# A written instruction order for ScalarE and VectorE, square sums moved to VectorE, and decay sums in fp32r, in a hybrid decoder step

## The chip, the cores and the metric

The kernel runs on one core of one Trainium2 chip. The metric is device time in microseconds. The engines are TensorE (PE, with its weight loads as PEld), VectorE (DVE), ScalarE (ACT), GpSimd (POOL) and SyncE (SP), which here only issues DMAs; ScalarE issues DMAs too.

## What is computed

One inference step of a hybrid autoregressive layer, for two groups that share the weights: a prompt of 256 tokens, and 8 samples of 8 tokens each with 1024 past positions in a paged cache. Model width is 1024, so 320 token columns pass through every projection.

```python
x += W_out[concat(MoBA heads, Mamba-2 SSD heads)](rmsnorm(x))
x += cross_attention(rmsnorm(x), rmsnorm(mem))
x += squared_relu_mlp(rmsnorm(x))

rmsnorm(x, g) = x * rsqrt(mean(x * x) + eps) * g

# Mamba-2 part, per chunk, with da = -dt * exp(a_log)
cum    = cumsum(da)
decay  = exp(where(causal, cum[l] - cum[s], -inf))
scores = einsum(C[l], B[s]) * decay
```

The step returns the outputs of both groups and the new keys, values, convolution rows, recurrent states and memory keys and values.

## The kernel before

All activations lie transposed, 128 model rows on the partitions and the 320 tokens in the free dimension. A weight chunk is 128x1024 fp32 (512 KB). `load` (L280) brings it in, on SyncE's queue or, for chunks 5 to 47, on ScalarE's. `chunk` splits it into a high part `wh` (ScalarE copy to fp32r, L332) and a low part `wl` (VectorE subtract, L333). The activations are split the same way by `split` (ScalarE L474, VectorE L475). `gemm3` (L338 to L340) then makes each product of three fp32r matmuls: high by high, high by low, low by high. Three raw, three high and three low chunk buffers exist, and two PSUM banks named `mm` for the gemms.

The program has a first part, in which many streams share TensorE, and a second, the MLP, which is gemms nearly throughout. The streams of the first part are: V and Q (value, query and key projections), F (their norms), S and T (sample and prompt attention), B and Z (convolution input and gate), D and R (the SSD scan), N (gated norm), O and J (the two halves of the output projection, `oa` and `os`), M, K and W (memory norms, keys and values), X (factors of the cross attention), a to d (cross attention), and G (its query and output projection, `ox`). Each stream is a generator; the string `ORDER` names, letter by letter, whose next piece is emitted, and that fixes TensorE's order. For the other engines the tile scheduler picks an order by priorities, when the program is built; on the chip each engine then runs its own list strictly in order.

Three places matter here.

- **Square sums.** A norm needs the sum of squares over 1024 model rows. `gather` (L433) squares each of the eight 128-row tiles on ScalarE (`square`, L423) and adds seven of them to the first on GpSimd, into `acc`. `means` (L442) copies the last 64 columns to fill the third 128-column tile (L439, GpSimd), then sums over the partitions with small matmuls. There are four such sums: of the input `x`, of the memory, of `x` after the output projection, and of `x` after the cross attention.
- **Decay sums.** `ssd_mix` (L997) scales a triangular matrix by each head's `da` into `rr`, on ScalarE, and one fp32 matmul for each 512 columns (L1013) against `gt` gives the differences of cumulative sums; ScalarE exponentiates them (L1014). The two prompt chunks have 1024 columns each, the sample chunk 512: five matmuls.
- **Row sums.** `sums` (L448) sums squares of heads by matmul, `rows_out` (L453) copies them out, and `transpose` (L316) turns them.

In the output projections the results leave PSUM on VectorE with the residual (`mix_done` L1268, `residual` L1282).

Of the kernel before, what the change touches and what calls it, by code (L numbers as in the profile page):

```python
# [47 lines left out]
for _n, _c in (("g_mix", 8), ("g_x", 8), ("g_mem", 8), ("g_mlp", 8), ("g_ssm", 4),  # L48
# [21 lines left out]
ORDER = ("VVVVQQQQQQQFQVQQQFQQVFVQQQQFQFQQQQFVQQQSSQQSQFQSQQQZQSSFSFSSSFFBFBSBBSBBZBBZBBSTZSSSBBBTBSSTBTBBBSBS"  # L70
         "BBSBSSBBSSSVTSSTZZSBBBSSTBZTBBBSSTBSSSZSDZDSTZDSDZDSSSDBDZDSSDZDDSSZZSDTSDDZRSSRSSRSSROMWROWRORROROO"
         "MNOOWZONONOWOOONONNOWOJJJJJJJJJJJMJJJWKJJKGWKKKKKKKJKKKKKKKaXMMGGGGGGMGGGGGGWGMGGGOcMXXbaaXccbaXdacb"
         "babcbaccddacddKbacddGGGGGGGGGGGGWGGGGG")
# [60 lines left out]
def _layout(a):  # L134
# [45 lines left out]
    for n, s in (("qg", f["q_norm_g"][0]), ("kg", f["k_norm_g"][0])):  # L180
# [12 lines left out]
        "ssm_s": (NB, P, 512), "mkT": (P, 4, 256), "mvo": (256, 512)}  # L193


def _body(tc, nc, I, O):
# [475 lines left out]
    def dt_part(tp):  # L672
# [26 lines left out]
        return dt, da  # L699
# [291 lines left out]
    def ssd_mix(t, bs_, tri, gt, n, out):  # L991
# [665 lines left out]
    for m in range(8):  # L1657
# [7 lines left out]
        S.dma_start(O["yT"][:, m, :], xT[:, m, :])  # L1665
    stD.close()
# [29 lines left out]
```

## Time and profile before

| | us |
|---|---|
| three runs | 532.46, 533.10, 533.56 (median 533.1) |
| the profiled execution | 533.69 |
| its span, first to last instruction | 531.9 |
| TensorE busy | 509.5 (96%) |
| VectorE busy | 342.5 (64%) |
| ScalarE busy | 251.9 (47%) |
| GpSimd busy | 79.2 (15%) |

The profile comes from one execution. TensorE's busy time is of pipelined matmuls with modelled ends, so overlapping lengths are listed longer than the step from one to the next. An idle time stands with the instruction that ended it, and with the releaser that came last. A tile name stands without its number, and a line number can be that of a helper that many places call.

### The profile page before, as it was taken

The numbers are of one execution on the slowest core, as the hardware profiler recorded it, in microseconds if no ns is written. First come the engines' busy times: TensorE is split into PE (matmuls) and PEld (weight loads), VectorE is DVE, ScalarE is ACT, GpSimd is POOL, SyncE is SP. The second block draws the span as 40 slices with busy tenths as digits, with TensorE's granted clock in tenths as the row PEclk, the third lists the DMA queues.
The fourth block names the chain that finished last, engine by engine and source line by source line (L and its number), as shares of the span: only waits on it lengthen the run. The fifth ranks groups of instructions, "written<-read, shape, count | busy, mean of one in ns | idle before, by whom it ended". The sixth has DMA issues, their size and how long they took to land.

```text
span 531.9 us, 10547 instructions
## 1 busy us (share of the span) xinstructions
PE 509.5 (96%) x3954; PEld 457.4 (86%) x3954; DVE 342.5 (64%) x677; ACT 251.9 (47%) x509; POOL 79.2 (15%) x126
## 2 busy tenths in 40 slices
PE   8899988999999999989899899999999999999997
PEld 6888577768667699879678899999999999999997
DVE  6858788677667788854647769776766533444331
ACT  8433536856666845552585443433433333223320
POOL 4700000110100310320002322322212100000000
PEclk9999999999999999998999899999999999999999
DMA  8799997979998235775942348464744455544530
GB/s 292 254 348 388 371 323 273 369 265 357 316 390 332 100 120 167 248 282 180 332 180 57 102 132 304 159 210 148 226 136 153 160 171 155 156 163 171 164 100 12
DMA packets 45365, 116.54 MB, mean 219 GB/s; under 512 B 5058, under 2 KB 7234, under 8 KB 45314
## 3 DMA queue, kind: packets, MB, share of 16 engines
q1 hardware_dynamic: 39266, 94.37, 52.0%
q10 hardware_dynamic: 6048, 21.50, 11.2%
q8 instruction: 31, 0.51, 0.4%
q14 instruction: 20, 0.16, 0.1%
HBM read 109.71 MB, written 6.14 MB: 218 GB/s over the span
## 4 chain that ended last, share of the span: by engine, by line
PE 80%; DVE 8%; ACT 7%; DMA 2%; issue 2%; SPq 1%; POOL 0%; ACTq 0%; DVEq 0%; POOLq 0%
PE mm L338 21%; PE mm L339 20%; PE mm L340 20%; ACT wh L332 3%; DVE wl L333 2%; PE sc L812 2%; PE as L865 2%; DVE big L475 2%; PE ms L316 2%; PE as L316 1%; PE sc L653 1%; DMA p<-memT 1%; DMA big<-xT 1%; PE as L1530 1%; PE as L1506 1%
## 5 line engine op out<-in xcount | busy, mean ns | idle before, releaser
L332 ACT ACTIVATE wh<-wr 128x1024 fp32r<-128x1024 f32 (+1 forms) x115 | 119.1, 1037 | 196.0 <-PE mm L339 128.2
L333 DVE TENSOR_TENSOR wl<-wr,wh 128x1024 fp32r<-128x1024 f32 (+1 forms) x115 | 146.0, 1272 | 95.8 <-ACT wh L332 94.4
L338 PE MATMUL mm<-big,wh 128*128 128x320 f32 x544 | 174.9, 322 | 3.2 <-DVE x2T L1282 1.4
L340 PE MATMUL mm<-big,wl 128*128 128x320 f32 x544 | 169.2, 311 | 1.4 <-DVE wl L333 1.4
L339 PE MATMUL mm<-big,wh 128*128 128x320 f32 x544 | 169.3, 311 | 0.0
L338 PEld LDWEIGHTS mm<-big,wh 128*128 128x128 f32 x544 | 103.3, 190 | 12.5 <-issue 8.7
L340 PEld LDWEIGHTS mm<-big,wl 128*128 128x128 f32 x544 | 103.4, 190 | 1.6 <-DVE wl L333 1.6
L339 PEld LDWEIGHTS mm<-big,wh 128*128 128x128 f32 x544 | 103.4, 190 | 0.6 <-issue 0.2
L340 PE MATMUL mm<-hh,wl 128*128 128x320 f32 x256 | 78.9, 308 | 0.0
L339 PE MATMUL mm<-hl,wh 128*128 128x320 f32 x256 | 78.9, 308 | 0.0
L338 PE MATMUL mm<-hh,wh 128*128 128x320 f32 x256 | 78.9, 308 | 0.0
L338 PEld LDWEIGHTS mm<-hh,wh 128*128 128x128 f32 x256 | 48.0, 188 | 0.0
L340 PEld LDWEIGHTS mm<-hh,wl 128*128 128x128 f32 x256 | 48.0, 188 | 0.0
L339 PEld LDWEIGHTS mm<-hl,wh 128*128 128x128 f32 x256 | 48.0, 188 | 0.0
L1619 POOL TENSOR_TENSOR t<-t 128x320 f32<-128x320 f32 x32 | 29.2, 912 | 88.1 <-DVE t L1616 79.2
L433 POOL TENSOR_TENSOR acc<-acc,sq 128x320 f32<-128x320 f32 x14 | 15.8, 1132 | 93.6 <-ACT sq L423 93.2
L1616 DVE SCALAR_TENSOR_TENSOR t<-mm,rb 128x320 f32<-128x320 f32 x32 | 15.6, 489 | 14.7 <-PE mm L340 13.6
L433 POOL TENSOR_TENSOR acc<-acc,t 128x320 f32<-128x320 f32 (+1 forms) x14 | 13.9, 995 | 41.5 <-ACT t L423 41.0
L1620 DVE TENSOR_TENSOR hl<-t,hh 128x320 fp32r<-128x320 f32 x32 | 15.4, 482 | 4.6 <-POOL t L1619 4.6
L812 PE MATMUL sc<-kv,qs 128*32 128x256 f32 x256 | 16.8, 382 | 0.2 <-DVE qs L602 0.2
L1617 ACT ACTIVATE hh<-t 128x320 fp32r<-128x320 f32 x32 | 14.7, 458 | 4.2 <-DVE t L1616 4.1
L865 PE MATMUL as<-kv,p 128*32 128x256 f32 x256 | 15.9, 382 | 0.0
(353 smaller groups left out, 635.7 us busy)
## 6 DMA issues: line engine op xcount, KB each, us to landing
wr<-w SPq DMA_DIRECT2D x69, 512.0 KB, 3.5
wr<-w ACTq DMA_DIRECT2D x41, 512.0 KB, 4.5
kv<-ckT SPq DMA_DIRECT2D x64, 256.0 KB, 5.1
kv<-cv SPq DMA_DIRECT2D x64, 256.0 KB, 5.9
kv<-mk SPq DMA_DIRECT2D x8, 512.0 KB, 4.4
kv<-mv SPq DMA_DIRECT2D x8, 512.0 KB, 5.0
kv<-h SPq DMA_DIRECT2D x4, 512.0 KB, 7.6
big<-h SPq DMA_DIRECT2D x4, 512.0 KB, 5.6
```

The source lines that it names most:

```text
L316: PE.transpose(out, in_, ident[:n, :n])
L332: A.activation(hi[:, c], raw[:, c], AF.Copy)
L333: V.tensor_tensor(lo[:, c], raw[:, c], hi[:, c], op=ALU.subtract)
L338: PE.matmul(out, hi[:, cols], xh, start=start, stop=False)
L339: PE.matmul(out, hi[:, cols], xl, start=False, stop=False)
L340: PE.matmul(out, lo[:, cols], xh, start=False, stop=stop)
L433: G.tensor_tensor(a, a, square(x, sq and sq()), op=ALU.add)
L812: PE.matmul(ps[r:r + 32, 256 * n:256 * n + 256], qs[:, s, g, b0 + e, :], kbs[e][:, :, 128 * (2 * g + s):128 * (2 * g + s) + 128], start=s ...
L865: PE.matmul(yv[r:r + 32, 0:256], pT[:, 2 * n + q, r:r + 32], vbs[e][:, q, 256 * g:256 * g + 256], start=n == 0 and q == 0, stop=first and ...
L1616: V.scalar_tensor_tensor(t, ps[:, :T], 0.0, rb3, op0=ALU.max, op1=ALU.mult)
L1619: G.tensor_tensor(f, t, t, op=ALU.mult)
L1620: V.tensor_tensor(hl[:, m, :], f, hh[:, m, :], op=ALU.subtract)
```

## The change

Five edits.

1. `ACT_ORDER` and `DVE_ORDER` list the places of all of ScalarE's and VectorE's instructions in the emitted program, DMA issues of ScalarE included ("3+1" is 3 and 4). At the end of `_body`, `_issue_order` ties each instruction to the one before it in the list, so that the scheduler must issue them so. SyncE and GpSimd stay with the scheduler.
2. `ORDER` is a new string: the pieces of TensorE's work come in another order.
3. `gather` adds on VectorE instead of GpSimd: 28 adds.
4. The padding of `acc` to 384 columns is a memset to 1 on GpSimd before the first square; for the input `x`, VectorE copies the last 64 columns.
5. In `ssd_mix`, `da` is split into `dah` and `dal`; ScalarE scales the triangular matrix by the high part (`rh`), VectorE by the low part (`rl`, one instruction for 512 columns), and two fp32r matmuls that accumulate take the place of each fp32 one. The halves of a prompt chunk are made one after the other, in two buffers; `gt` is copied to fp32r.

```diff
-ORDER = ("VVVVQQQQQQQFQVQQQFQQVFVQQQQFQFQQQQFVQQQSSQQSQFQSQQQZQSSFSFSSSFFBFBSBBSBBZBBZBBSTZSSSBBBTBSSTBTBBBSBS"
+ORDER = ("VVFVVQQQQQQQQQQQQQQQVFVQFVQFFQQQQFVQQQQQSSQQQFSSQQZQZQSSFSFSSSFFBBBBSZBBSBBFSBBTZSBSSBBBSSTBBTBTBBSS"
...
+ACT_ORDER = ("1 0 2 19 3+1 20 6 5 7 21 8+3 22 12+3 23 16+2 24+2 28 30 33 32 27 37 34 29 43 38 31 50 39 44 36 35 53 59 40+1 "
...
+DVE_ORDER = ("0+2 17 4 3 5 18 6+7 19 14+1 20 16 21+2 27 32 24 35 25+1 36 28 30 29 31 53 33+1 37 39 38 40+8 54 73 49 51 50 52 "
...
+def _issue_order(tc, nc, eng, runs):
+    ins = [i for i in nc.cur_bb.bb.instructions if i.engine == eng and i.is_tile_traced]
+    ins = [ins[i] for i in _runs(runs)]
+    info = mybir.DependencyInfo(mybir.DependencyClass.NoSync, mybir.DependencyReason.DATA)
+    for a, b in zip(ins, ins[1:]):
+        tc.add_manual_dep(b, a.name, info, reason="issue order")
...
     def gather(acc, x, sq=None):
         if not acc:
+            n = x.shape[-1]
             acc.append(tl(tp_, [P, 384], "acc", bufs=2))
-            square(x, acc[0][:, :x.shape[-1]])
+            if n % P:
+                G.memset(acc[0][:, n:P * -(-n // P)], 1.0)
+            square(x, acc[0][:, :n])
         else:
             a = acc[0][:, :x.shape[-1]]
-            G.tensor_tensor(a, a, square(x, sq and sq()), op=ALU.add)
+            V.tensor_tensor(a, a, square(x, sq and sq()), op=ALU.add)
...
-        if n % P:
-            G.tensor_copy(a[:, n:P * nt], a[:, n - 64:n])
...
     def x_squares():
         for kt in range(8):
             gather(xsq, xT[:, kt, :], lambda: tm(T))
+        V.tensor_copy(xsq[0][:, T:], xsq[0][:, TP:T])
...
+        dah, dal = [tl(p1, [P, 24], n, F32R) for n in ("dah", "dal")]
+        V.tensor_copy(dah, da)
+        V.tensor_tensor(dal, da, dah, op=ALU.subtract)
...
-        for h in range(8):
-            A.activation(rr[:, h, :], tri, AF.Copy, scale=dat[:, h:h + 1])
+        gtr = tl(made["sb"], [P, P], "es", F32R)
+        A.activation(gtr, gt, AF.Copy)
+        hn = 512 // n
+        def expand(h0):
+            rh, rl = [tl(made["sb"], [P, hn, n], "rx", F32R, bufs=2) for _ in range(2)]
+            for h in range(hn):
+                A.activation(rh[:, h, :], tri, AF.Copy, scale=dah[:, h0 + h:h0 + h + 1])
+            V.tensor_tensor(rl, tri[:, None, :].broadcast_to((P, hn, n)), dal[:, h0:h0 + hn, None].broadcast_to((P, hn, n)), op=ALU.mult)
+            return rh, rl
+        rx = expand(0)
...
-        for c in range(0, 8 * n, 512):
+        for h in range(0, 8, hn):
+            if h:
+                rx = expand(h)
+                yield 0.5, 2.0
             sg = ms()
-            PE.matmul(sg, gt, rf[:, c:c + 512], start=True, stop=True)
-            A.activation(df[:, c:c + 512], sg, AF.Exp)
+            for i, r in enumerate(rx):
+                PE.matmul(sg, gtr, r.rearrange("p h l -> p (h l)"), start=i == 0, stop=i == 1)
+            A.activation(rr[:, h:h + hn, :], sg.rearrange("p (h l) -> p h l", h=hn), AF.Exp)
...
+    for eng, runs in ((mybir.EngineType.Activation, ACT_ORDER), (mybir.EngineType.DVE, DVE_ORDER)):
+        if runs:
+            _issue_order(tc, nc, eng, runs)
```

Line numbers of the changed program are higher by 35 to 70: L333 becomes L384, L442 L494, L448 L500, L475 L527, L720 L776, L1282 L1349.

VectorE at the end of the `ox` stage, before: `x2T` is the residual, `wl` the low part of the next weight chunk, `big` the low part of the split.

```order
L475 SCALAR_TENSOR_TENSOR big_3735<-x2T_2845,prm_81,big_3735 128x320
L1282 TENSOR_TENSOR x2T_2845<-mm_3873,qs_2526 128x320
L1282 TENSOR_TENSOR x2T_2845<-mm_3892,kv_2527 128x320
L333 TENSOR_TENSOR wl_4020<-wr_4017,wh_4019 128x1024
L475 SCALAR_TENSOR_TENSOR big_3735<-x2T_2845,prm_81,big_3735 128x320 x2
L443 TENSOR_SCALAR ti_3938<-ms_3940 128x3
```

And in the changed program, where `acc` is the square sum:

```order
L1349 TENSOR_TENSOR x2T_2880<-mm_3902,qs_2533 128x320
L527 SCALAR_TENSOR_TENSOR big_3763<-x2T_2880,prm_81,big_3763 128x320
L1349 TENSOR_TENSOR x2T_2880<-mm_3921,kv_2534 128x320
L487 TENSOR_TENSOR acc_3786<-acc_3786,sq_3918 128x320
L384 TENSOR_TENSOR wl_4048<-wr_4045,wh_4047 128x1024
L487 TENSOR_TENSOR acc_3786<-acc_3786,sq_3937 128x320
L527 SCALAR_TENSOR_TENSOR big_3763<-x2T_2880,prm_81,big_3763 128x320 x2
L495 TENSOR_SCALAR ti_3967<-ms_3968 128x3
```

The adds stand between residual, low part and the last two splits, which are last in both.

TensorE at the end of the memory keys, before: the last gemm matmuls on `kv`, the square sum's matmuls, the row sums of the key squares `t`, and the transposes of their copy `s`.

```order
L339 MATMUL mm_3183<-kv_2555,wh_3186 128x256
L340 MATMUL mm_3183<-kv_2554,wl_3187 128x256
L442 MATMUL ms_3227<-cst_82,acc_2903 128x8 x3
L448 MATMUL ms_3234<-t_3214,cst_82 32x256
L448 MATMUL ms_3234<-t_3180,cst_82 32x256
L448 MATMUL ms_3234<-t_3146,cst_82 32x256
L448 MATMUL ms_3234<-t_3112,cst_82 32x256
L316 MATMUL ms_3241<-cst_82,s_578_3239 128x128 x2
L338 MATMUL mm_3260<-big_2900,wh_3263 128x320
L339 MATMUL mm_3260<-big_2900,wh_3263 128x320
```

And in the changed program (`sc` is the memory value projection W):

```order
L1549 MATMUL sc_2582<-wh_3235,kv_2552 128x512
L1550 MATMUL sc_2582<-wl_3236,kv_2552 128x512
L1551 MATMUL sc_2582<-wh_3235,kv_2553 128x512
L1549 MATMUL sc_2582<-wh_3235,kv_2552 128x512
L1550 MATMUL sc_2582<-wl_3236,kv_2552 128x512
L1551 MATMUL sc_2582<-wh_3235,kv_2553 128x512
L500 MATMUL ms_3245<-t_3230,cst_82 32x256
L500 MATMUL ms_3245<-t_3196,cst_82 32x256
L500 MATMUL ms_3245<-t_3162,cst_82 32x256
L500 MATMUL ms_3245<-t_3128,cst_82 32x256
L494 MATMUL ms_3253<-cst_82,acc_2931 128x8 x3
L389 MATMUL mm_3261<-big_2928,wh_3264 128x320
```

Six matmuls of W have come ahead of the row sums, the square sum's matmuls behind them; the transposes of `s` follow only after six matmuls of the next gemm.

VectorE at the first prompt scores, before: the mask is added to four score tiles (`tq`) and their maxima are taken (`pmx`).

```order
L720 TENSOR_TENSOR tq_1126<-ms_1103,cst_82 128x384
L720 TENSOR_TENSOR tq_1129<-ms_1104,cst_82 128x384
L721 TENSOR_REDUCE pmx_197_1123<-tq_1126 128x3
L721 TENSOR_REDUCE pmx_197_1123<-tq_1129 128x3
L720 TENSOR_TENSOR tq_1134<-as_1105,cst_82 128x384
L725 TENSOR_TENSOR pmx_197_1123<-pmx_197_1123 128x2
L720 TENSOR_TENSOR tq_1137<-as_1106,cst_82 128x384
L726 SCALAR_TENSOR_TENSOR pmx_1124<-pmx_197_1123,fqs_176 128x4
L333 TENSOR_TENSOR wl_1411<-wr_1408,wh_1410 128x1024
L721 TENSOR_REDUCE pmx_197_1123<-tq_1134 128x3
L721 TENSOR_REDUCE pmx_197_1123<-tq_1137 128x3
```

And in the changed program:

```order
L776 TENSOR_TENSOR tq_1131<-ms_1108,cst_82 128x384
L776 TENSOR_TENSOR tq_1134<-ms_1109,cst_82 128x384
L776 TENSOR_TENSOR tq_1139<-as_1110,cst_82 128x384
L776 TENSOR_TENSOR tq_1142<-as_1111,cst_82 128x384
L1013 SCALAR_TENSOR_TENSOR t_1172<-mm_767,rb_179 128x320
L777 TENSOR_REDUCE pmx_199_1128<-tq_1134 128x3
L777 TENSOR_REDUCE pmx_199_1128<-tq_1131 128x3
L777 TENSOR_REDUCE pmx_199_1128<-tq_1142 128x3
```

All four adds, two of which empty the PSUM banks `as`, now come ahead of the maxima; the weight's low part has moved behind them.

## Rows read from the trace of the kernel before

**Rows 1.** Windows: microseconds; busy time (instructions) of each engine, granted clock, DMA share, GB/s.
```profile
0.00:300.00 300.00, 280.98 (x2392) 230.25 (x2392) 217.62 (x517) 174.44 (x415) 49.99 (x94) 0.99 0.75 267
300.00:528.00 228.00, 228.00 (x1562) 226.89 (x1562) 124.36 (x159) 77.42 (x94) 29.26 (x33) 0.99 0.49 159
```

**Rows 2.** TensorE's waits: line, releaser and its line; total us, times, longest us.
```profile
PE ms L448 <- ACT sq L423: 1.8, 2, 1.3
PE ms L442 <- POOL acc L433: 1.5, 1, 1.5
PE mm L338 <- DVE x2T L1282: 1.4, 3, 0.6
PE mm L340 <- DVE wl L333: 1.4, 1, 1.4
...
PE as L316 <- ACT p L837: 1.2, 3, 0.6
PE as L316 <- DVE tq L720: 1.2, 1, 1.2
PE ms L316 <- ACT s L453: 1.1, 2, 0.6
PE mm L338 <- DVE kv L1366: 1.1, 1, 1.1
PE ms L448 <- ACT t L423: 1.0, 1, 1.0
...
PE ms L316 <- ACT tq L742: 0.6, 1, 0.6
...
PE as L316 <- ACT yn L900: 0.6, 1, 0.6
```

**Rows 3.** Timeline of TensorE: start us, length us, instruction [idle before it <- releaser].
```profile
238.40 0.64 PE L448 MATMUL ms<-t,cst 128*32 128x256 f32 x8 [1.01 <-ACT t L423]
...
299.70 0.50 PE L442 MATMUL ms<-cst,acc 128*128 128x8 f32 x3 [1.51 <-POOL acc L433]
```

**Rows 4.** Windows of TensorE alone: busy time (matmuls), granted clock, DMA share, GB/s.
```profile
239.00:244.00 5.00, 4.47 (x24) 0.66 0.98 379
...
240.00:242.00 2.00, 2.00 (x10) 0.50 1.03 422
...
256.00:262.00 6.00, 4.12 (x30) 1.00 0.99 338
...
300.00:305.00 5.00, 5.00 (x26) 0.66 0.16 66
```

**Rows 5.** The chain that ended last, pieces of TensorE: start us, us, what.
```profile
22.93 1.38 PE sc L653 x6
...
148.34 1.91 PE ms L1013 x4
```

**Rows 6.** Line L433 on GpSimd (window); two VectorE groups by form: busy us, mean ns.
```profile
0.00:300.00 300.00, 29.78 (x28) 0.99 0.75 267
...
L1620 DVE TENSOR_TENSOR hl<-t,hh 128x320 fp32r<-128x320 f32 x32 | 15.4, 482 | 4.6 <-POOL t L1619 4.6
...
L1023 DVE TENSOR_TENSOR rr<-rr,gm 128x512 f32<-128x512 f32 x4 | 2.8, 689 | 1.4 <-ACT rr L1014 1.4
```

**Rows 7.** Timelines of VectorE and GpSimd in the `ox` stage.
```profile
284.74 1.22 DVE L333 TENSOR_TENSOR wl<-wr,wh 128x1024 fp32r<-128x1024 f32 x1 [0.46 <-ACT wh L332]
285.88 1.17 DVE L475 SCALAR_TENSOR_TENSOR big<-x2T,prm,big 128x320 fp32r<-128x320 f32 x1
286.98 0.88 DVE L1282 TENSOR_TENSOR x2T<-mm,kT 128x320 f32<-128x320 f32 x2
288.09 0.55 DVE L475 SCALAR_TENSOR_TENSOR big<-x2T,prm,big 128x320 fp32r<-128x320 f32 x1 [0.23 <-ACT big L474]
290.18 1.17 DVE L475 SCALAR_TENSOR_TENSOR big<-x2T,prm,big 128x320 fp32r<-128x320 f32 x1
...
297.55 2.09 POOL L433 TENSOR_TENSOR acc<-acc,sq 128x320 f32<-128x320 f32 x2 [1.19 <-ACT sq L423]
```

More of the change, by code (lines that the diff above doesn't have):

```diff
@@ L69 @@
 PACE = 1.3
-ORDER = ("VVVVQQQQQQQFQVQQQFQQVFVQQQQFQFQQQQFVQQQSSQQSQFQSQQQZQSSFSFSSSFFBFBSBBSBBZBBZBBSTZSSSBBBTBSSTBTBBBSBS"
-         "BBSBSSBBSSSVTSSTZZSBBBSSTBZTBBBSSTBSSSZSDZDSTZDSDZDSSSDBDZDSSDZDDSSZZSDTSDDZRSSRSSRSSROMWROWRORROROO"
-         "MNOOWZONONOWOOONONNOWOJJJJJJJJJJJMJJJWKJJKGWKKKKKKKJKKKKKKKaXMMGGGGGGMGGGGGGWGMGGGOcMXXbaaXccbaXdacb"
-         "babcbaccddacddKbacddGGGGGGGGGGGGWGGGGG")
+ORDER = ("VVFVVQQQQQQQQQQQQQQQVFVQFVQFFQQQQFVQQQQQSSQQQFSSQQZQZQSSFSFSSSFFBBBBSZBBSBBFSBBTZSBSSBBBSSTBBTBTBBSS"
+         "BSBSVBBSSSSBTSSTBZSZBBSSTTBBBSZBBTSTBSSDZSDZSZDDZSSDSSTSDZDDSSDDDZZDDSDSZDRSZSSSRSSRDSSMRWROORWRROMR"
+         "NWOOOZWOONONOOOOOOONNNWOJJJJMJJJJJJJJJJWJKJKKJKKKKKKKKKKKKKWMXGGMGGcGGGaOGGMGGGGWGGGGMXbXaKacXccXbad"
+         "cabbabbcaMbcddacdadcddGGGGGGGGGGGGGGGGWG")
+ACT_ORDER = ("1 0 2 19 3+1 20 6 5 7 21 8+3 22 12+3 23 16+2 24+2 28 30 33 32 27 37 34 29 43 38 31 50 39 44 36 35 53 59 40+1 "
[14 rows of a table added]
+DVE_ORDER = ("0+2 17 4 3 5 18 6+7 19 14+1 20 16 21+2 27 32 24 35 25+1 36 28 30 29 31 53 33+1 37 39 38 40+8 54 73 49 51 50 52 "
[19 rows of a table added]
 TAKEN = []
@@ L193, with _runs @@
         "ssm_s": (NB, P, 512), "mkT": (P, 4, 256), "mvo": (256, 512)}
+def _runs(s):
+    out = []
+    for r in s.split():
+        a, _, n = r.partition("+")
+        out += range(int(a), int(a) + int(n or 0) + 1)
+    return out
+def _issue_order(tc, nc, eng, runs):
[4 more added lines that the diff above has]
+        tc.add_manual_dep(b, a.name, info, reason="issue order")
 def _body(tc, nc, I, O):
@@ L994, in ssd_mix @@
         dat = dts[1][:, 8 * t:8 * t + 8]
-        rr = tl(made["sb"], [P, 8, n], "rr", bufs=2)
-        for h in range(8):
-            A.activation(rr[:, h, :], tri, AF.Copy, scale=dat[:, h:h + 1])
-        rf = rr.rearrange("p h l -> p (h l)")
+        dah, dal = [d[:, 8 * t:8 * t + 8] for d in dts[2:]]
+        gtr = tl(made["sb"], [P, P], "es", F32R)
[8 more added lines that the diff above has]
+        rx = expand(0)
         gp = ms()
@@ L1008, in ssd_mix @@
         yield 0.55, 2.5
-        dec = tl(made["sb"], [P, 8, n], "rr", bufs=2)
-        df = dec.rearrange("p h l -> p (h l)")
-        for c in range(0, 8 * n, 512):
+        rr = tl(made["sb"], [P, 8, n], "rr")
+        for h in range(0, 8, hn):
+            if h:
+                rx = expand(h)
+                yield 0.5, 2.0
             sg = ms()
-            PE.matmul(sg, gt, rf[:, c:c + 512], start=True, stop=True)
-            A.activation(df[:, c:c + 512], sg, AF.Exp)
+            for i, r in enumerate(rx):
+                PE.matmul(sg, gtr, r.rearrange("p h l -> p (h l)"), start=i == 0, stop=i == 1)
+            A.activation(rr[:, h:h + hn, :], sg.rearrange("p (h l) -> p h l", h=hn), AF.Exp)
         tail = tl(p1, [P, 8], "tail")
         if n == P:
-            V.tensor_copy(tail, dec[:, :, n - 1])
+            V.tensor_copy(tail, rr[:, :, n - 1])
         else:
@@ L1022, in ssd_mix @@
         for g in range(2):
-            V.tensor_tensor(rr[:, 4 * g:4 * g + 4, :], dec[:, 4 * g:4 * g + 4, :], gm[:, g:g + 1, :].broadcast_to((P, 4, n)), op=ALU.mult)
+            V.tensor_tensor(rr[:, 4 * g:4 * g + 4, :], rr[:, 4 * g:4 * g + 4, :], gm[:, g:g + 1, :].broadcast_to((P, 4, n)), op=ALU.mult)
         out += [a, rr, tail, dab]
@@ L1032, in ssd_y @@
                 PE.matmul(ec[:, n * j:n * j + n], dab[:, 128 * j:128 * j + 128], tri, start=True, stop=True)
-            es = tl(made["sb"], [P, 4 * n], "es%d" % n).rearrange("p (j l) -> p j l", j=4)
+            es = tl(made["sb"], [P, 4 * n], "es").rearrange("p (j l) -> p j l", j=4)
             A.activation(es, ec[:, 0:4 * n].rearrange("p (j l) -> p j l", j=4), AF.Exp)
```

2 lines of the change are left out of this document (1 added, 1 removed), and 33 rows, old and new, of tables (ACT_ORDER, DVE_ORDER).

## The prediction

> **What bounds the kernel now.** I read the windows first. From 300 to 528 us TensorE is busy for all 228.0 us [rows 1]: the reader is to see that nothing done on other engines can shorten that part except through its clock. From 0 to 300 us it is busy for 280.98, so 19.0 us are idle [rows 1]; 1.35 of them precede the first warm-up matmul. That first part is where the change works. VectorE is busy 217.6 of those 300 us and ScalarE 174.4: neither is full, so an order on them matters where TensorE waits for one particular result.
>
> The list of TensorE's waits says which results [rows 2]. No DMA is in it. The entries are short, and each is one place in the program: a square that a row-sum matmul needs, a softmax tile that a transpose needs, a PSUM bank that VectorE has not emptied. The timeline places two of them [rows 3]: one at 238.4 us, just before the next for a row copy (half of L453's 1.1 [rows 2]), and the one behind GpSimd's sums at 299.7 us.
>
> The third view is the granted clock [rows 4]. In 239 to 244 us its mean is 0.66, in 240 to 242 it is 0.50 (the 1.2 GHz level), and in 300 to 305 us it is 0.66 again. The first fall follows those two waits of 1.01 and about 0.5 us; the second follows the waits of the `ox` stage and the one of 1.51 us [rows 2, 3]. Each costs 5 x 0.34 = 1.7 us. But 256 to 262 us, with only 4.12 of 6 us busy, kept 1.00 [rows 4]: idle time alone does not tell when the clock falls.
>
> **The change, part by part.** The sum is made against the profiled execution, 533.69 us, of which 531.9 is its span; the median of the three runs, 533.1, is 0.6 lower.
>
> *Decay sums.* Five fp32 matmuls of 512 columns go, ten fp32r ones come. Two fp32 ones took 1.91 us, 0.955 each [rows 5]; six fp32r ones of 512 columns took 1.38, 0.23 each [rows 5]. So 4.78 us become 2.30: **-2.5 us**, on TensorE itself, while it has little slack. The low parts are five VectorE products of 128x512, 0.69 each by the nearest row [rows 6] (3.4 us); ScalarE's eight scalings per tile stay. The second half of a tile waits for the first half's matmuls, because one pair of buffers serves both; the new order puts six gemm matmuls, eight value matmuls and four more between them, which covers it.
>
> *Square sums.* Twenty-eight GpSimd adds go, GpSimd's 29.8 us of line L433 [rows 6]. On VectorE an add of 320 columns from SBUF takes 0.48 [rows 6], so 21 of them and 7 shorter ones (I take 0.42) are 13.0 us. With the products above and the small splits VectorE gets 16.9 us more. It also gets something back: in the `ox` stage the subtract of the split takes 0.55 alone and 1.17 while a GpSimd add runs [rows 7]. The Trainium skill, "SBUF — State Buffer", section "SBUF: two separate sides", says that a VectorE instruction with two SBUF inputs and a GpSimd instruction that reads SBUF lock each other out for a whole instruction. By that rule the moved adds would give back up to 29.8 us, an estimate from the whole length of the adds, and VectorE would be lighter than before; the two stage terms below would then stand at their lower ends (-1.9 and -1.4), and the sum 519.0. The trace agrees that the two collide. It shows 0.62 for a collision, not the 1.1 of an add, so I keep to the rows.
>
> *Waits that the orders take away.* A gemm matmul is one of the 320-column ones at 0.145 us (20 us hold 138 of them in the full stretch, as 1562 in 228 us [rows 1]).
> - Start: the low half of the first q chunk waits 1.4 [rows 2] behind VectorE's subtracts. Those lose their GpSimd neighbours and one copy moves behind; three adds come in between. **-1.1** (0 to -1.4).
> - 30 to 175 us, named places. Exponentials of the first sample pair: 1.2 in three waits, six more gemm matmuls (0.87) ahead: -0.9. Prompt scores: four mask adds now run in a row, two reduces of about 0.5 move behind, wait 1.2: -0.9. Prompt probabilities, 0.6 (L742): sixteen score matmuls move ahead: -0.6. `yn`, 0.6: six gemm matmuls ahead: -0.6. q's row sums, 1.8 less 1.3, so 0.45: eight value matmuls ahead: -0.45 [all rows 2]. Against that: the transposes behind q's row sums lose their cover of six matmuls, which I price at the like waits of L453, about 0.5 each [rows 2]; and the exponentials at about 134 us have 18 instead of 30 gemm matmuls ahead, 1.74 us less cover, of which only half the tile is needed at once: +0.8. Together **-2.1** (0 to -4).
> - `os` stage, 207 to 231 us: VectorE-released waits, the largest 1.1 (L1366) [rows 2]. The adds come in, the collisions go: **-0.6** (+1.5 to -1.9).
> - Memory factors: six `W` matmuls of 0.23 now stand between the last k gemm and its row sums, and six gemm matmuls between the sums and the transposes. That is 1.38 and 0.87 us of cover against 1.01 and about 0.5 [rows 2, 3]: **-1.5** (0 to -1.5).
> - Cross factors, the 1.3 and the remaining half of 1.1 [rows 2]: four short transposes and four score matmuls move in between: **-1.0** (0 to -1.9).
> - `ox` stage: 1.4 in three waits [rows 2] on the VectorE residual. There VectorE's cycle per weight chunk is 4.3 us (290.18 less 285.88 [rows 7]) while TensorE's is 24 x 0.145 = 3.5. After: 1.14 for the low part (285.88 less 284.74), 0.88 for two residuals, at most 2 x 0.55 for two subtracts that run alone and 2 x 0.48 for two adds make some 4.0, by start-to-start times, which are shorter by 0.1, 3.8 [rows 6, 7]: **-1.0** (0 to -1.4).
> - Square sums at 299.7 us: 1.51 [rows 3]. Two GpSimd adds (2.09 us) and a copy stood behind the last square [rows 7]; now one add of 0.48 does, placed ahead of the last two subtracts: **-1.3**.
>
> *The clock.* If the waits at 238 to 240 and 287 to 300 us go, I expect both falls to go: **-3.4** (0 to -3.4).
>
> *New waits.* VectorE carries 16.9 us more in a first part where its results already cost TensorE 5.1 us of waits (its four entries in [rows 2]). By proportion that is 0.4; at worst I take a quarter of 16.9, 4. I put **+1.5**. Every instruction of ScalarE, the weight-load issues on its queue among them, now also stands behind its written predecessor; SyncE's queue moves only a few issues (the x reload goes six page loads and four state loads later, a value store earlier), and TensorE waits for no DMA now, so I cost these at nothing; the loads' cover is the buffered chunks, and if that were gone see the rival that is slower.
>
> Sum: -2.5 - 1.1 - 2.1 - 0.6 - 1.5 - 1.0 - 1.0 - 1.3 - 3.4 + 1.5 = -13.0, so 533.7 - 13.0 = **520.7 us**.
>
> **Rivals.**
> 1. *The clock falls elsewhere.* For it: 256 to 262 us shows that idle time and falls do not match one to one. Against: both falls stand right behind the largest clusters of waits. Time 520.7 + 3.4 = 524.1. The Trainium skill, "TensorE: Matmul & The Clock Gate", section "A second HAM failure mode: psum-queue depth-cycling", says that frequent small idles between groups of matmuls can make the clock swing; many small idles are what remains here, and the trace agrees in that no single long idle stands before either fall. Chance 0.18.
> 2. *Waits only move.* The chain behind each result stays as long, and the next instruction waits in place of this one: only the matmul saving, the start and the sums at 299.7 stay, with one clock fall gone: 533.7 - 2.5 - 1.1 - 1.3 - 1.7 + 1.5 = 528.6. For it: many links in these chains are latencies that no order shortens. Chance 0.14.
> 3. *Deeper.* VectorE's load costs nothing (1.5 us) and the terms of 30 to 175 us and of the cross factors reach their lower ends (1.9 and 0.9 more): 520.7 - 4.3 = 516.4. For it: VectorE is idle for 82 of the first 300 us [rows 1]. Chance 0.10.
> 4. *Slower: weight loads in a written order.* ScalarE issues 41 of the weight loads (512 KB each). In a fixed order an issue behind an activation that waits for TensorE comes late, and the chunk's high half, low half and gemm follow it. Price: 41 loads times what each is late at TensorE. It decides from 13.0 + 1.1 = 14.1 us on, that is 0.34 us for each load; at 0.4 the time is 533.7 - 13.0 + 16.4 = 537.1. For it: DMA share was 0.98 to 1.03 in the short windows near 240 us [rows 4]. Against: no DMA in TensorE's waits, and the order before was as fixed on the chip. Chance 0.06.
> 5. *fp32r gains nothing here.* Ten matmuls at the fp32 price would add 4.8 instead of saving 2.5: 520.7 + 7.3 = 528.0. Against: 0.23 us for the same shape in this kernel. Chance 0.02.
>
> **How the numbers follow.** My forecast, with every term near its value, has 0.50. A measurement of this kernel can tell about 0.2%, 1.1 us, from no change. Faster by more than that are the forecast, rivals 1, 3 and 5 and nearly all of rival 2: 0.90. Same: 0.04, the worst of rival 2. Slower: 0.06. The range takes in the deeper case with a little more, since several terms have lower ends, and the clock and the worst of the new waits above: 514.5 to 528.6; what lies outside is part of rival 2, the slower case and some of rival 3, about 0.2.
>
> **What would show it.** Right: L448 of the k sums and L442 at the end of `ox` without a wait over 0.3 us; granted clock 1.00 around both; the decay matmuls at about 0.46 us a pair; GpSimd without the adds; the split's subtract at 0.55 throughout; idle before 300 us at about 10 us. Wrong: a DMA or `wh` in TensorE's list of waits, idle at 16 us or more before 300 us, or the part from 300 us on longer than 229 us.

## The result, and the profile after

The changed kernel takes 518.66 us, median of four runs (518.02 to 520.65), against 532.93 for the kernel before: a ratio of 0.9738, 95% interval 0.9709 to 0.9767. The forecast was 520.7 us. The profiled execution took 520.65, with a span of 518.9 us, and is the slowest of the four; the other three have spans of 516.2 to 517.3.

The windows of the profile after, with the columns of [rows 1]:

```profile
0.00:300.00 300.00, 285.66 (x2472) 239.47 (x2473) 225.47 (x572) 179.08 (x425) 22.93 (x69) 1.00 0.76 271
300.00:515.00 215.00, 215.00 (x1482) 213.91 (x1482) 117.45 (x141) 72.38 (x87) 25.52 (x29) 1.00 0.50 163
```

TensorE idles for 14.3 of the first 300 us in place of 19.0 [rows 1], and the granted clock is 1.00 in both stretches: neither fall of before is left in this execution. Over the whole span, span less TensorE's busy time went from 22.4 (531.9 - 509.5) to 17.8 us (518.9 - 501.1), that is 4.6 less, and the busy time fell by 8.4. Of the 8.4, the clock is 3.4 and the decay about 1.6 (its five pairs of matmuls stand below); 3.4 are left over, and no term of the prediction had them.

TensorE's waits after, the longest, to be read against [rows 2]:

```profile
PE sc L868 <- DVE m L872: 2.3, 2, 1.8
PE ms L1065 <- DVE big L1003: 1.7, 1, 1.7
PE ms L534 <- POOL ts L531: 1.4, 1, 1.4
PE as L367 <- ACT p L893: 1.3, 3, 0.5
PE ms L494 <- DVE acc L487: 1.1, 1, 1.1
PE ms L500 <- ACT sq L474: 0.9, 1, 0.9
```

The waits on `wl`, on the convolution `kv`, on the memory's row copy and on the residual `x2T` are gone. At the top stand two that did not exist before. The timeline shows where they are, and the sum's wait that answers to [rows 3]:

```profile
122.29 1.06 PE L868 MATMUL sc<-kv,qs 128*32 128x256 f32 x14 [1.77 <-DVE m L872]
...
144.44 0.49 PE L1065 MATMUL ms<-big 128*128 128x128 f32 x2 [1.69 <-DVE big L1003]
...
288.17 0.83 PE L494 MATMUL ms<-cst,acc 128*128 128x8 f32 x6 [1.09 <-DVE acc L487]
```

ScalarE's timeline ahead of the two (an `ACTq` row is a DMA issue on ScalarE's queue):

```profile
115.93 0.33 ACTq L331 DMA_DIRECT2D wr<-w  x1
116.39 0.67 ACT L994 ACTIVATE t<-t,cwh 128x344 f32<-128x344 f32 x1 [3.69 <-DMA kv<-ckT]
...
143.06 0.33 ACTq L331 DMA_DIRECT2D wr<-w  x1
143.44 0.49 ACT L998 ACTIVATE t<-t 128x344 f32<-128x344 f32 x1 [3.44 <-DMA kv<-ckT]
```

Both times ScalarE stands still for over 3 us in front of a weight-load issue, which goes only when a key page of the cache has landed; a convolution activation stands right behind it. The chain of waits says the same of the second:

```profile
138.42 4.55 DMA kv<-ckT
...
143.06 0.33 ACTq L331
143.39 0.05 issue
143.44 0.50 ACT t L998
143.94 0.02 issue
143.96 0.44 DVE big L1003
144.40 0.04 issue
144.44 0.49 PE ms L1065 x2
144.93 0.47 PE ms L1080 x2
```

For the first, VectorE's timeline has the link: it waits 3.87 us for that activation, then has a queue of prompt scores ahead of the maximum (L872). That one has to read the sample scores' PSUM tile, of which there is one, before TensorE writes the next scores there.

```profile
113.01 0.21 DVE L848 TENSOR_REDUCE m<-po 128x1 f32<-128x64 f32 x1
117.09 0.58 DVE L996 SCALAR_TENSOR_TENSOR t<-t,cwh,t 128x344 f32<-128x344 f32 x1 [3.87 <-ACT t L994]
...
121.56 0.68 DVE L872 TENSOR_REDUCE m<-sc 128x2 f32<-128x512 f32 x1
```

When the same kernel was traced again (changed_again below), the first of the two waits was 0.74 us and the second 1.68: the first changes from execution to execution.

The decay's other four pairs in the chain (the first is in the piece above), against [rows 5]:

```profile
147.71 0.66 PE ms L1080 x2
...
157.32 0.73 PE ms L1080 x2
159.81 0.59 PE ms L1080 x2
...
176.62 0.47 PE ms L1080 x2
```

### The profile page after: what moved, and what is told of

Its sections match the earlier page's. It is cut to its first block, busy times and chain, and to the rows that moved or that the text cites. A ratio compares the mean times of both kernels' runs of the same rounds, so it can differ in the third digit from the quotient of the medians.

```text
span 518.9 us, 10547 instructions
## 1 busy us (share of the span) xinstructions
PE 501.1 (97%) x3954; PEld 453.6 (87%) x3954; DVE 343.4 (66%) x713; ACT 251.5 (48%) x512; POOL 48.4 (9%) x98
## 4 chain that ended last, share of the span: by engine, by line
PE 78%; DVE 8%; ACT 6%; DMA 5%; issue 2%; SPq 0%; ACTq 0%; POOL 0%; POOLq 0%
PE mm L389 21%; PE mm L390 20%; PE mm L391 20%; DMA kv<-ckT 3%; PE ms L367 2%; ACT wh L383 2%; DVE wl L384 2%; DMA wr<-w 2%; PE as L921 2%; PE sc L706 1%; PE as L367 1%; PE ms L534 1%; PE sc L868 1%; PE mm L1623 1%; PE sc L1549 1%
## 5 line engine op out<-in xcount | busy, mean ns | idle before, releaser
L384 DVE TENSOR_TENSOR wl<-wr,wh 128x1024 fp32r<-128x1024 f32 (+1 forms) x115 | 144.7, 1261 | 83.5 <-ACT wh L383 81.0
L389 PE MATMUL mm<-big,wh 128*128 128x320 f32 x544 | 171.9, 316 | 2.4 <-DVE t L881 0.7
L390 PE MATMUL mm<-big,wh 128*128 128x320 f32 x544 | 168.2, 309 | 0.0
L389 PEld LDWEIGHTS mm<-big,wh 128*128 128x128 f32 x544 | 102.2, 188 | 9.6 <-issue 5.7
L390 PEld LDWEIGHTS mm<-big,wh 128*128 128x128 f32 x544 | 102.2, 188 | 0.8 <-DVE big L1611 0.3
L391 PEld LDWEIGHTS mm<-big,wl 128*128 128x128 f32 x544 | 102.1, 188 | 0.2 <-DVE wl L384 0.2
L1686 POOL TENSOR_TENSOR t<-t 128x320 f32<-128x320 f32 x32 | 27.8, 869 | 171.3 <-DVE t L1683 162.4
L996 DVE SCALAR_TENSOR_TENSOR t<-t,cwh,t 128x344 f32<-128x344 f32 x24 | 13.8, 573 | 7.7 <-ACT t L994 7.3
L868 PE MATMUL sc<-kv,qs 128*32 128x256 f32 x256 | 15.9, 381 | 2.3 <-DVE m L872 2.3
L1349 DVE TENSOR_TENSOR x2T<-mm,x2T 128x320 f32<-128x320 f32 x8 | 3.9, 492 | 17.8 <-PE mm L391 17.8
```

What stands on the lines that cost most here:

```text
L384: V.tensor_tensor(lo[:, c], raw[:, c], hi[:, c], op=ALU.subtract)
L389: PE.matmul(out, hi[:, cols], xh, start=start, stop=False)
L390: PE.matmul(out, hi[:, cols], xl, start=False, stop=False)
L391: PE.matmul(out, lo[:, cols], xh, start=False, stop=stop)
L868: PE.matmul(ps[r:r + 32, 256 * n:256 * n + 256], qs[:, s, g, b0 + e, :], kbs[e][:, :, 128 * (2 * g + s):128 * (2 * g + s) + 128], start=s ...
L1686: G.tensor_tensor(f, t, t, op=ALU.mult)
```

## The experiments

Three questions were open: which part of the change carries the gain; whether the two new waits come from the place of the load issues in the written order; and what the adds are worth on VectorE. Each kernel was timed against the kernel before on the same chip; single runs of one kernel spread there by 1% and more, so the ratios and the traces carry more than the medians. Idle is the profiled span less TensorE's busy time.

| kernel | what differs | ratio to before (95%) | idle, us | mean clock |
|---|---|---|---|---|
| before | | 1 | 22.4 | 0.994 |
| adds_only | before, adds on VectorE | 1.0002 (0.9978 to 1.0027) | 22.7 | 0.994 |
| decay_only | fp32r decay and padding; TensorE's order of before, no written orders | 1.0175 (1.0135 to 1.0215) | 31.6 | 0.984 |
| old_pe_order | the same and adds on VectorE | 1.0155 (1.0109 to 1.0202) | 30.9 | 0.987 |
| no_orders | the same with TensorE's new order | 1.0283 (1.0234 to 1.0333) | 37.6 | 0.980 |
| no_orders_pool | no_orders, adds on GpSimd | 1.0352 (1.0316 to 1.0389) | 40.6 | 0.978 |
| no_act_order | VectorE's written order added | 1.0264 (1.0208 to 1.0319) | 39.2 | 0.984 |
| no_dve_order | ScalarE's written order added | 1.0119 (1.0074 to 1.0165) | 30.5 | 0.990 |
| changed_again | both: the changed kernel | 0.9742 (0.9693 to 0.9792) | 16.7 | 1.000 |
| pool_adds | the changed kernel, adds on GpSimd | 0.9863 (0.9814 to 0.9912) | 20.0 | 0.997 |
| late_loads | the changed kernel, two load issues later | 0.9683 (0.9640 to 0.9726) | 15.2 | 0.999 |
| later_loads | three load issues later | 0.9678 (0.9636 to 0.9720) | 16.0 | 1.000 |
| third_load | the third later still | 0.9636 (0.9610 to 0.9662) | 13.6 | 1.000 |

### The written orders taken away

no_orders leaves both strings empty; no_act_order and no_dve_order leave one empty.

```diff
-ACT_ORDER = ("1 0 2 19 3+1 20 6 5 7 21 8+3 22 ...
+ACT_ORDER = ("")
-DVE_ORDER = ("0+2 17 4 3 5 18 6+7 19 14+1 20 ...
+DVE_ORDER = ("")
```

> The changed kernel with both written orders left empty, so that the scheduler orders ScalarE and VectorE; TensorE's order is the new one, instruction for instruction, and the adds and the decay stay changed. Theory 1 (what the prediction's terms rest on, the orders take waits away): TensorE's idle before 300 us rises from 14 us to 18 us or more and at least one fall of the clock comes back, 523 to 527 us. Theory 2 (TensorE's order, the moved adds and the decay carry the gain, and the written orders only repeat the scheduler): 518 to 519.5 us. Theory 3 (the written orders cost: two weight-load issues of ScalarE wait 3.4 and 3.7 us for page loads, and TensorE waits 1.7 and 1.8 behind them): without them 515 to 516 us.

> Only ScalarE's written order is left empty; VectorE's and TensorE's stay, instruction for instruction. If ScalarE's order carries a part of the gain (theory 1): 520 to 524 us, with new waits of TensorE on ScalarE's rows (exponentials, yn, row sums). If it only costs (theory 3): the waits of 1.8 us on the maxima (L872) and 1.7 us on the convolution (L1003) go, 515 to 516 us. If it matters neither way (theory 2): 518 to 519.5 us.

> Only VectorE's written order is left empty; ScalarE's and TensorE's stay. Theory 1: VectorE's order is what holds the adds and subtracts in front of the waits, so 520 to 525 us, with the waits on x2T (L1349) and on the sums (L494) back at 1 us or more. Theory 2: 518 to 519.5 us.

Measured: 550.12, 549.92 and 541.41 us. Theory 1 has the direction, but every figure in it was far too small: without the orders the kernel is not 4 to 8 but some 30 us slower than with them, and slower than the kernel before. ScalarE's order alone brings back 1.6% (1.0283 to 1.0119), VectorE's alone nothing that can be told (1.0264); the two together bring 5.4%. They are one thing. In no_dve_order the waits that theory 1 named are back, 1.46 us on `x2T` (L1349) and 1.83 on the sums (L494).

Of the 29.4 us between the spans of no_orders (548.3) and the changed kernel, 19.8 are idle time; the rest is busy time, much of it the clock, whose mean is 0.980 there and 1.000 in the changed kernel. One place shows both. ScalarE in no_orders:

```profile
104.46 0.67 ACT L994 ACTIVATE t<-t,cwh 128x344 f32<-128x344 f32 x1 [0.29 <-issue]
105.16 0.47 ACT L893 ACTIVATE p<-sc,b 128x256 f32<-128x256 f32 x1
...
107.30 0.49 ACT L998 ACTIVATE t<-t 128x344 f32<-128x344 f32 x1
107.68 0.87 ACT L798 ACTIVATE tq<-ms 128x384 f32<-128x384 f32 x2
```

TensorE's timeline there:

```profile
108.23 1.11 PE L367 MATMUL ms<-cst,tq 128*128 128x128 f32 x4 [4.61 <-ACT tq L798]
```

and the windows of no_orders around it:

```profile
100.00:108.00 8.00, 2.96 (x19) 2.46 (x17) 6.26 (x21) 6.83 (x21) 1.03 (x6) 0.91 0.95 352
108.00:112.00 4.00, 3.77 (x16) 3.78 (x17) 2.62 (x8) 2.63 (x6) 0.25 (x3) 0.50 0.57 183
```

The scheduler puts the exponentials of the sample scores (L893) and a convolution product ahead of the copies of the transposed prompt scores out of PSUM (L798). TensorE's new order has the next transposes first and stands still for 4.61 us; behind it the clock is granted at 0.50. In the changed kernel the first of these copies starts at 94.58 us, ahead of the exponentials, and TensorE's only wait from 92 to 104 us is one of 0.26. Each order is good or bad only with the others.

no_orders_pool is no_orders with the adds on GpSimd (the edit stands below).

> As no_orders, with the adds back on GpSimd. If the adds in the scheduler's order are what makes it 31 us slower than the changed kernel: 530 to 540 us. If it is TensorE's new order, which needs ScalarE's and VectorE's results in the written order: 546 to 552 us, with the waits on tq (L798) and kv (L1433) of 3 us or more still there.

Measured: 554.62 us, a ratio of 1.0352. The adds are not what makes no_orders slow; without the move it is no faster.

### The parts under TensorE's order of before

adds_only is the kernel before with one letter changed. old_pe_order is the changed kernel with TensorE's `ORDER` of before (the decay's two extra pieces, one for each prompt chunk, directly behind the ones that they belong to) and no written orders; decay_only is the same with the adds on GpSimd.

```diff
-            G.tensor_tensor(a, a, square(x, sq and sq()), op=ALU.add)
+            V.tensor_tensor(a, a, square(x, sq and sq()), op=ALU.add)
```

> The kernel before, with its 28 adds of square sums on VectorE and nothing else changed (TensorE's order is that of before, the scheduler orders the rest). If the adds by themselves shorten the waits, as the prediction's terms for the start and for the sums at 300 us say: 530 to 533 us against 533. If in an order that is not written for them they make VectorE late (what the 542.9 us of old_pe_order would need): 536 us or more, with longer waits on VectorE's rows at 200 to 230 and 287 to 310 us. If the decay alone is at fault there: 533 us.

> As old_pe_order, with the adds back on GpSimd: what is left of the change is the fp32r decay (and the padding by a constant). The prediction's term: 2.5 us faster than before, 530.5 us. If the new chain behind the decay (ScalarE's four copies and VectorE's product for each half, then the exponential, two halves in turn) is not covered by TensorE's order of before: the waits at 148 to 192 us stay, some 7 us in place of 0.75, so 2.5 less, 7 more and a fall of the clock or two, 538 to 542 us.

> The changed kernel with TensorE's order of before (the two new pieces of the decay follow each other at once) and both written orders left empty: what stays of the change is the adds on VectorE and the fp32r decay. Theory 1a (TensorE's new order was made for the written orders and is bad without them; the adds and the decay are worth what the prediction says): 533 less 2.5 for the decay and about 1.3 for the sums at 300 us, so 528 to 530 us, some 20 us less than the kernel without orders. Rival 1b (the adds make VectorE late in any order that is not written out, and the new order of TensorE is not at fault): 540 us or more.

Measured: 534.41, 544.92 and 542.90 us. The adds by themselves do nothing for the time, but they move waits. In the trace of adds_only the start's wait on `wl` is 0.16 us in place of 1.37, and `x2T` has 0.69 in place of 1.38; the sums at 300 us wait 1.97 in place of 1.51, and a new wait of 1.72 us stands at 194 us, ahead of row sums (L448). Behind it the clock falls, and it no longer falls at 240 us, as two windows of adds_only show (in the kernel before they have 1.00 and 0.70):

```profile
195.00:200.00 5.00, 5.00 (x24) 4.74 (x22) 1.84 (x10) 0.55 (x2) 0.00 (x0) 0.66 0.38 105
240.00:245.00 5.00, 4.18 (x33) 3.70 (x34) 3.50 (x15) 0.63 (x2) 0.00 (x0) 1.00 0.71 239
```

The prediction put the decay at 2.5 us faster; decay_only is 1.75% slower than before, some 9 us. Not all of that is the decay's: two waits on `wl`, 1.62 and 1.82 us at 16 and 22 us, where the kernel before has one of 1.37, come ahead of any decay matmul, and in the profiled execution the clock falls five times, not twice. The price that theory 1a gives to the decay falls with it. The other half of 1a stands: with TensorE's new order and no written orders the same code is slower still (1.0283 against 1.0155, and 1.0352 against 1.0175). Rival 1b has old_pe_order's time but not its reason, since the adds are not at fault. The timeline of TensorE in decay_only shows the waits around the decay:

```profile
155.21 1.02 PE L1080 MATMUL ms<-rx,es 128*128 128x512 f32 x2 [1.62 <-ACT rx L1059]
...
170.15 0.73 PE L1080 MATMUL ms<-rx,es 128*128 128x512 f32 x2 [1.61 <-DVE t L886]
...
173.72 1.16 PE L1148 MATMUL ms<-big,hst 128*128 128x128 f32 x8 [1.95 <-ACT rr L1081]
```

and ScalarE's the reason for the first: the four copies for the second half, one ahead of an exponential and three behind it, are made only after the first half's matmuls (at 152.85 us), because there is one pair of `rx` buffers.

```profile
153.40 0.40 ACT L1059 ACTIVATE rx<-cst,dah 128x128 fp32r<-128x128 f32 x1
153.70 0.58 ACT L1081 ACTIVATE rr<-ms 128x512 f32<-128x512 f32 x1
154.18 0.97 ACT L1059 ACTIVATE rx<-cst,dah 128x128 fp32r<-128x128 f32 x3
```

For the third, the scheduler's order has five exponentials of the sample scores (L893, L896) ahead of the one that TensorE waits for (L1081, at 173.07 us). In the kernel before, the second chunk's eight copies (L997) were made from 151.8 to 155 us, and its matmuls began at 160.7. From 130 to 175 us the listed waits add up to 6.1 us in decay_only and 0.75 before. TensorE's new order puts other matmuls between the halves; in the changed kernel no decay matmul (L1080) is in the list of waits. The new decay also has one `rr` buffer where there were two, and shares the buffer of `es`; what these cost was not tried apart. Nor was the changed kernel run with the fp32 decay, or with written orders for TensorE's order of before, so the decay's worth within the whole is read from the trace alone.

### The adds, within the changed kernel

pool_adds has the 28 adds back on GpSimd and VectorE's written order without them.

> The changed kernel with its 28 adds of square sums back on GpSimd; VectorE's written order is the same without them, ScalarE's and TensorE's orders stay. The prediction's terms for the start (1.1), the memory stage's collisions (0.6), the residual stage (1.0) and the sums at 300 us (1.3) rest on the move of the adds: 520.5 to 523 us. Rival (VectorE's load is what the new waits come from): 516 to 518 us.

Measured: 526.25 us, where changed_again on the same chip took 520.37: 5.9 us, more than was expected; of the spans it is 4.7 (522.3 - 517.6). One place makes 2.3 of it: GpSimd's last three adds of the sum of `x` run from 18.71 to 21.51 us, VectorE's copy of `acc` (L618) waits for them, and the first q chunk stands behind that in VectorE's order. Their squares are there at 14.1 us; the adds are late because the scheduler put eight small products (L566, 13.40 to 18.75 us) ahead of them on GpSimd. So this part is a matter of order again, more than a price of the adds. VectorE's timeline, and TensorE's:

```profile
21.55 0.20 DVE L618 COPY acc<-acc 128x64 f32<-128x64 f32 x1 [3.82 <-POOL b L884]
```
```profile
24.02 0.38 PE L389 MATMUL mm<-big,wh 128*128 128x320 f32 x1 [2.66 <-DVE qz L585]
```

Another 1.7 is the clock, which is at 0.66 from 145 to 150 us. A window inside it:

```profile
145.00:148.00 3.00, 2.76 (x10) 2.55 (x10) 1.84 (x5) 1.94 (x7) 0.00 (x0) 0.56 0.99 369
```

It stands behind a wait of 2.03 us at 145.24; the changed kernel, with 1.69 us at the same place, has no fall there. The other five executions of pool_adds have mean clocks of 0.987 to 0.997 where the profiled one has 0.997, so falls are a larger part of the 5.9 us than of the 4.7.

The places that the expectation named hardly change. The sums at the end of the `ox` stage wait 1.22 us in place of 1.09, and no wait on `x2T` is listed in either kernel: within the written orders these two terms do not rest on the adds.

> The changed kernel itself, for a comparison on this chip: a ratio of 0.971 to 0.977 to the kernel before.

It repeats: 0.9742. But two of its six executions have a mean clock of 0.993 and 0.997 (523.43 and 522.11 us), so the clock can fall in the changed kernel too.

VectorE's load is the finding here. The groups by form have the split's subtract in the `ox` stage (busy us, mean ns); in the kernel before:

```profile
L475 DVE SCALAR_TENSOR_TENSOR big<-x2T,prm,big 128x320 fp32r<-128x320 f32 x8 | 7.4, 933 | 1.1 <-ACT big L474 1.1
```

in the changed kernel:

```profile
L527 DVE SCALAR_TENSOR_TENSOR big<-x2T,prm,big 128x320 fp32r<-128x320 f32 x8 | 4.3, 543 | 1.0 <-ACT big L526 1.0
```

in pool_adds:

```profile
L527 DVE SCALAR_TENSOR_TENSOR big<-x2T,prm,big 128x320 fp32r<-128x320 f32 x8 | 5.5, 692 | 1.0 <-ACT big L526 1.0
```

The page gives VectorE 343.4 us busy with the adds and 341.0 without them. The adds take 13.0 us on VectorE (6.7 + 3.4 + 2.9 in the three forms of L487), and raise its busy time by 2.4. Part of the 10.6 between is only that the listed lengths of neighbouring instructions overlap. With all lengths added up, VectorE's other instructions take 7.3 us less than in pool_adds, 0.26 for each add; 3.1 of it is the split's subtract and 1.3 the weights' low part. adds_only shows the same with nothing else changed: this subtract takes 548 ns there in place of 933, and VectorE is busy for 341.9 us with the adds, against 342.5 without.

### The weight-load issues

late_loads moves two entries of ScalarE's order, here as the instructions stand:

```diff
+L994 ACTIVATE t_1575<-t_1568,cwh_158 128x344
 L331 DMA wr_2584<-w 128x1024
-L994 ACTIVATE t_1575<-t_1568,cwh_158 128x344
...
-L331 DMA wr_2736<-w 128x1024
 L998 ACTIVATE t_1922<-t_1917 128x344
 L1015 ACTIVATE t_1986<-t_1984 128x320
 L1185 ACTIVATE sq_2398<-big_84 128x8x8
+L331 DMA wr_2736<-w 128x1024
 L1059 ACTIVATE rx_2060<-cst_82,dah_891 128x128 x4
```

> Two entries of ScalarE's written order move: the weight-load issue that waited 3.7 us goes one place later, behind the convolution product (L994), and the one that waited 3.4 us goes three places later, behind L998, L1015 and L1185; all other engines keep their order. Theory 3 (these two issues, which wait for a page load to land, hold up the activations behind them, and these hold up TensorE): the waits of 1.8 us (L868 on m L872) and 1.7 us (L1065 on big L1003) go, 515.2 us, 3.4 less than the changed kernel. Rival (the waits only move: VectorE is full at 118 us anyway, and the next link is late): 517.5 to 518.7 us, with a wait of over 1 us at 120 to 124 us or 142 to 146 us.

Measured: 517.99 us, a ratio of 0.9683; changed_again has 0.9742, on another chip and with intervals that overlap, so the traces must decide. Both waits are gone. But the second issue goes only at 141.70 us, and now the decay's copies stand behind it. ScalarE's timeline and TensorE's:

```profile
141.70 0.34 ACTq L331 DMA_DIRECT2D wr<-w  x1
142.08 1.28 ACT L1059 ACTIVATE rx<-cst,dah 128x128 fp32r<-128x128 f32 x4 [3.29 <-PE as L854]
```
```profile
143.41 0.73 PE L1080 MATMUL ms<-rx,es 128*128 128x512 f32 x2 [1.40 <-ACT rx L1059]
```

The row of the copies names a matmul that ended just before they started. That it was the issue which held them shows in later_loads: there it no longer stands in front of them, and the same copies start at 139.47 us.

later_loads puts that issue behind the second half's exponential (L1081), and a third one behind the second tile's first exponential. third_load moves only the third further:

```diff
 L1081 ACTIVATE rr_2300<-ms_2301 128x512
-L331 DMA wr_2803<-w 128x1024
 L1059 ACTIVATE rx_2305<-cst_82,dah_891 128x128 x2
 L1059 ACTIVATE rx_2564<-cst_82,dah_891 128x64
 L1081 ACTIVATE rr_2300<-ms_2331 128x512
+L331 DMA wr_2803<-w 128x1024
 L893 ACTIVATE p_2268,sm_2267<-sc_2155,b_383_2255 128x256 x2
```

> As late_loads, where the second weight-load issue, put ahead of the decay's copies (L1059), now held those up and cost TensorE 1.4 us at 143 us; here it goes behind them, six places further, and a third issue goes three places later, behind the copies of the second tile (0.4 us at 154 us). If a load issue that waits delays just what stands behind it: both waits go, 1.5 to 1.8 us less than late_loads, a ratio of about 0.965 to the kernel before. Rival (the chunk that is loaded later now comes late itself): a wait of TensorE on wh or wl (L389, L391) at 148 to 165 us, and no gain over late_loads.

Measured: 517.33 us, no gain that can be told. The 1.40 us are gone, and the third issue, held until a value page landed at 155.2, took their place with 2.26 us at 156 us, again through L1059. The mechanism held and the place was wrong once more.

> As later_loads, with the third weight-load issue behind all of the second tile's copies and exponentials (L1059, L1081): there it waited until 155.2 us for a page load of 7.1 us and cost TensorE 2.3 us at 156 us. If a late issue only delays what stands behind it: that wait goes, 1.5 to 2.3 us less than later_loads, a ratio of about 0.964. Rival (the next thing behind it, the exponentials of the sample scores, L893, is late instead): no gain, with a wait of over 1 us between 156 and 165 us.

Measured: 515.36 us, 0.9636. The listed waits from 130 to 175 us are now none, where the changed kernel has 1.69. Its longest waits:

```profile
PE ms L534 <- POOL ts L531: 1.4, 1, 1.4
PE sc L868 <- DVE m L872: 1.3, 1, 1.3
PE ms L494 <- DVE acc L487: 1.1, 1, 1.1
```

Its interval ends at 0.9662, below the 0.9709 at which that of the changed kernel's first measurement begins: three entries out of 507 are worth about 1%, 5 us. The two waits that they took away are 3.46 us of it by the first trace of the changed kernel and 2.42 by that of changed_again. Some of the rest is the clock, which stayed at 0.999 or 1.000 in all six executions. The wait on L872 that is left stands at 55 us, not at 122. It is the fastest kernel here.

## Why the prediction was right, and where it was not

The time was right, 520.7 against 518.66, and so was the sign. That the two profiled executions differ by just the 13.0 us of the sum is luck: single terms are off by up to 4 us and balance. Term by term, from the profiled executions:

- **Decay, -2.5.** Measured about -1.6. Only two of the five pairs take 0.47 in the chain, as said; with 0.66, 0.73 and 0.59 they make 2.9 us. Before, two tiles took 1.91 and 1.78 and the last 0.86 from start to start, 4.55. The saving also needs the cover that the term named: decay_only has no such cover and waits 5.4 us more from 130 to 175 us. The term was a saving of the whole change, not of the part.
- **Start, -1.1.** Measured: the 1.4 on `wl` gone, 0.35 new at 21.5 us; -1.0.
- **30 to 175 us, -2.1.** Wrong in sign. The listed waits there went from 7.15 to 9.06 us, +1.9. The named places did shrink (the prompt scores, 1.2 to 0.5; the prompt probabilities and `yn`, none left), except the exponentials (L893), still 1.3; q's row sums lost their 0.45, but the transposes behind them wait 0.72; the two load issues added 3.46. Without those the stretch would be at -1.6.
- **`os` stage, -0.6.** No wait is left there; before, 1.96 us were listed between 207 and 231 us. The lower end, -1.9, was the better value.
- **Memory factors, -1.5.** The two waits are gone: -1.5. In changed_again's trace 0.78 is listed at the row sums.
- **Cross factors, -1.0.** 1.3 and 0.56 became 0.9: -1.0.
- **`ox` stage, -1.0.** No wait on `x2T` is left: -1.4. The subtract runs at 0.54 throughout, as said; but pool_adds, where it takes 0.69, has no wait on `x2T` either.
- **Square sums, -1.3.** Measured -0.4, 1.51 to 1.09 us. The add is fast, but the written order put a weight split (L384, 1.23 us, from 286.48) ahead of the last add.
- **Clock, -3.4.** Both falls are gone from the profiled execution, -3.4.
- **New waits, +1.5.** The size was too small and the cause was another. VectorE was not the source: it is busy 343.4 us against 342.5, where the prediction added 16.9. The adds and the products are 16.5 us of work, and with all lengths added up VectorE has 5.8 us more than before, so some 11 us came back in shorter instructions, 8.0 of them in the split's low part (L475). The Trainium skill, "SBUF — State Buffer", section "SBUF: two separate sides", says that a VectorE instruction with two SBUF inputs and a GpSimd one that reads SBUF shut each other out for a whole instruction. The trace agrees: with the adds gone the subtract fell from 933 to 543 ns. I kept to one collision of 0.62, and should have asked how many there are: a VectorE lighter than before, which I set aside, is what adds_only has. The largest new waits came from ScalarE; two smaller ones, 0.67 and 0.59 at 257 and 271 us, are in the cross attention.
- **Rival 4, weight loads in a written order.** It was costed as a delay of the chunk that is loaded. What the runs show in its place is a delay of what stands behind the issue on ScalarE: no wait of TensorE in the changed kernel is on a weight chunk, and two of the 41 issues cost 3.5 us through activations (2.4 in changed_again's trace). "TensorE waits for no DMA now, so I cost these at nothing" is the step that failed: an issue can itself wait for a DMA, and then ScalarE waits with it.

So the waits fell by 4.6 us where the terms without decay and clock make 7.1, and the decay gave 0.9 less than its term. These 3.4 us were made up by 3.4 us of busy time that no term had. Taking each matmul's start to the next one's, less idle, up to the sums of the last norm, the transposes (L367) take 1.6 us less, the sample scores (L868) 0.8 and the prompt scores (L768) 0.5, while two others (L1119, L1623) take 0.5 more each. That matmuls follow each other more closely in the new order is the likely cause, but it was not tried, and the rest of the 3.4 is not traced.

Of the signs that the prediction named, the k sums without a wait, the clock and the subtract came as said in this execution. The sums at the end of `ox` still wait 1.09 us, not under 0.3, and the idle time before 300 us is 14.3 us, between its marks of 10 and 16.

Rival 1 (the clock falls elsewhere) did not come in the profiled execution of the changed kernel; adds_only shows that it happens, and two of changed_again's executions have falls somewhere. The Trainium skill, "TensorE: Matmul & The Clock Gate", section "A second HAM failure mode: psum-queue depth-cycling", says that many small idles can make the clock swing. The trace of the changed kernel does not show it: 19 waits of 0.17 to 1.77 us in the first 300, and no fall.

## What to carry to other kernels

Orders written for several engines are one object: with the same code and the same order on TensorE, leaving ScalarE's and VectorE's to the scheduler cost 30 us, of which one list alone brought back 9 and the other nothing, so price them together and test the parts only within the whole. When a DMA issue shares a queue with compute, look at what that issue waits for and put it behind whatever is needed sooner; three such moves were worth 1% here. A faster instruction that is fed from a smaller buffer can cost more in waits than it saves, unless the order puts other work between its halves.

## What was not expected of the hardware

A window shows a mean clock of 0.56 behind a wait of 2.03 us (pool_adds), while 1.77 and 1.69 us, at 122 and 144 us, left it at 1.00 in the changed kernel; before, falls came behind 1.01 with 0.5 and behind 1.51 us. The length of the last wait alone does not order these cases. Nor does the kernel: executions of the kernel before have mean clocks from 0.987 to 0.997. And the adds, 13.0 us of work for VectorE, made it busy for only 2.4 us more in the changed kernel, and for 0.6 less in adds_only.
